# A Mamba/pooling decoder step on one core: the first gate tile multiplied from raw rows, and a new order of the first loads

## The chip, the cores and the metric

The kernel runs on one core of one Trainium2 chip. The metric is the device time of one execution in microseconds (us), the median of several runs. The engines are named as the profile names them: PE (TensorE, matmuls; PEld are its weight loads), DVE (VectorE), ACT (ScalarE), POOL (GpSimd) and SP (SyncE, which here only issues DMAs; SPq in the profile). Each engine runs its instructions in the order in which the program gives them, and waits for others at semaphores.

## The reference, cut to what matters

The model step has two layers, a Mamba-2 layer and a pooling layer, for 1024 prompt tokens and 8 samples of 8 tokens, 1088 tokens of 1024 features in all. Each layer first makes a modulated, normed input and projects it:

```
mod = silu(c) @ ada_w + ada_b;  shift, scale, gate = split(mod, 3)
hn  = rmsnorm(x, norm_g) * (1 + scale) + shift
zxbcdt = hn @ w_in            # z: 2048 gate columns, then x/B/C and dt
...                           # conv, state-space scan, y * silu(z), ...
```

`scale` and `shift` have one row for the prompt and one for each sample. Only the front of the first layer is touched: `mod` for layer 0, the norm, `hn`, and the first of the sixteen tiles (128 columns each) of `silu(z)`. All inputs and results are fp32.

## The kernel before, in words

Features lie on the 128 partitions and tokens along the free dimension, so `x` is eight tiles of 128x1088 (`xs[0]` to `xs[7]`). An exact product is made of three matmuls in the fp32r format: each operand is split in a rounded part (`hi`, ACT) and the rest (`lo`, DVE), and `mm1` (L182 to L186) adds hi*hi (L184), hi*lo (L185) and lo*hi (L186). A column tile of `w_in` against all of `hn` is thus 8 feature tiles x 3 token chunks (368, 368 and 352 columns) x 3 = 72 matmuls.

What the front does before the change, in its order:

- **Loads** (`setup`, L196, and `front`, L1338), all on SP's queue: the conditioning `cT`, the eight `x` tiles (L203), the constants `vec` and `kc` (L206, L208), the weight for dt (`wdt`), and then, two transfers each, the adaLN weights of layer 0 (`ada`, L251) in eight blocks, with the first weight tiles (`wr`, L121) behind the first block.
- **Warming**: 55 fp32 matmuls of 128 columns on a tile of ones (L220 calls `warm`, its matmul is L239).
- **1/rms**: ACT squares each `x` tile as it lands (L1347, L1351), DVE adds them up in `rst` (L1352), three fp32 matmuls with ones sum over the partitions (L295, tiles `ms`), and ACT makes 1/rms with Ln and Exp (L298, L311).
- **adaLN**: `ada_block` (L242) multiplies one block by the conditioning, as 2 x 4 fp32 matmuls in four column strips (L255, tiles `am`), copies the sum (L260), and picks nine columns with two more matmuls (L264). DVE then makes `shf` (L273) and `scl` (L274). One block gives shift and scale of one feature tile.
- **The loop over k** (L1372 to L1386 of `front`): for each of the eight feature tiles `modulate` (L313) makes `hn`: DVE multiplies by scale and 1/rms (L318), ACT adds the shift and rounds (L324, the hi part `hh`), DVE takes the rest (L325, `hl`), ACT writes `hn` back over `x` (L326), and the 64 sample tokens get their own small operations (L331 to L335). The 18 matmuls of two gate tiles (2 x 3 chunks x 3) and the dt matmuls (L1384) of that k follow. Gate tiles 0 and 1 so grow together in six PSUM banks.
- **Gate tiles 2 and 3** are then made one after the other (L1395 to L1402), 72 matmuls each. Meanwhile `act_sums_front` (L1405) makes the sums and differences of `hn` that the next stage needs (DVE subtractions at L1412, splits on ACT at L1415 and DVE at L1416), and `dt_phase` (L443) works on dt.
- **`front_pairs`** (L1446) makes all further tiles in pairs by seven half-size products instead of eight (`fast_pair`, L1022; matmuls L1017 to L1019, tiles `st`). The sums of weights for it are made by POOL (`w_sums`, L982 to L989), which also takes the rest of some splits (L178; ACT's rounding is L176). A raw weight tile (`wr`) is one of three buffers, and the next load into a buffer waits until its readers are done.

What sets the order around the change: the program order and `issue_after` marks feed a scheduler, so an engine's queue isn't the order of the code. In SP's queue a transfer that must wait holds up those behind it.

The lines of the program before that the steps below speak of most:

```
def ada_first(self, kt):                               # one block: shift and scale of tile kt
    for _ in self.ada_shift_scale(0, kt, False): pass
...
self.ada_first(0); ...; self.ada_first(1)              # ahead of the loop over k
for k in range(8):
    if k < 6: self.ada_first(k + 2)
```

## Time and profile before

| | |
|---|---|
| time, median of 3 runs | 1612.11 us (1608.94 to 1612.48) |
| the profiled execution | 1608.36 us; its span, first to last instruction, 1606.6 us |
| mean granted TensorE clock | 0.996 |
| PE busy | 1579.4 us (98% of the span) |
| DVE, ACT, POOL busy | 1292.8 us, 790.0 us, 506.7 us |
| first matmul of the exact product | 23.77 us after the span's start |
| last dt matmul group of the loop over k begins | 68.39 us |

The profile is one execution. All times within it count from the first instruction. "PE busy" counts a matmul from its start to its modelled end, so a full PE isn't a PE at its peak; where it waits shows in the idle time ahead of an instruction and in what ended it. The granted clock is that of PE, as a share of full speed.

### The profile page before, as it was taken

How to read it: one execution, taken by the hardware profiler on the slowest of the kernel's cores; microseconds unless marked ns; L12 is line 12 of the kernel's file. 1: busy time of each engine (PE TensorE's matmuls, PEld its weight loads, DVE VectorE, ACT ScalarE, POOL GpSimd, SP SyncE). 2: the span in 40 equal slices, each digit the busy share in tenths (PEclk: the TensorE clock that was granted, in tenths of full speed). 3: DMA queues.
4: the chain of work that ended last, by engine and by line, in shares of the span. 5: the costliest groups of instructions: out<-in, count | busy, mean ns of one | idle time of the engine just before them, and what ended most of it. 6: DMA issues, size and time to landing. Idle time of an engine off the chain costs nothing.

```text
span 1606.6 us, 30635 instructions
## 1 busy us (share of the span) xinstructions
PE 1579.4 (98%) x11916; PEld 1505.1 (94%) x11916; DVE 1292.8 (80%) x2148; ACT 790.0 (49%) x1511; POOL 506.7 (32%) x562
## 2 busy tenths in 40 slices
PE   8999999999999999999999999999999999999997
PEld 6899999998889889888899898999999999999997
DVE  6975779778888888888888967988889867677886
ACT  6663343447676666675545437632232233333364
POOL 0133556522221312130212222275666640000241
PEclk9999999999999999999999999999999999999999
DMA  9422232354555454768898632133323379565783
GB/s 351 166 100 84 95 111 71 109 185 150 198 166 174 151 199 144 245 214 303 287 330 292 221 133 86 57 131 114 115 101 101 116 232 364 161 171 177 161 177 119
DMA packets 122305, 275.58 MB, mean 172 GB/s; under 512 B 18192, under 2 KB 59312, under 8 KB 122160
## 3 DMA queue, kind: packets, MB, share of 16 engines
q1 hardware_dynamic: 118128, 260.90, 47.1%
q0 software_dynamic: 4032, 12.72, 4.5%
q8 instruction: 94, 1.54, 0.4%
q14 instruction: 51, 0.42, 0.1%
HBM read 201.12 MB, written 70.23 MB: 169 GB/s over the span
## 4 chain that ended last, share of the span: by engine, by line
PE 84%; DVE 6%; issue 4%; ACT 2%; DMA 2%; POOL 2%; SPq 0%; DVEq 0%; ACTq 0%; POOLq 0%
PE mm L184 11%; PE mm L185 10%; PE mm L186 10%; PE st L1019 10%; PE st L1017 10%; PE st L1018 10%; PE op L1234 3%; PE op L1235 3%; PE op L1233 3%; PE y L625 2%; PE S L604 2%; PE y L629 2%; PE tr L565 1%; PE am L255 1%; DVE xbc L352 1%
## 5 line engine op out<-in xcount | busy, mean ns | idle before, releaser
L1017 PE MATMUL st<-hh,w 128*128 128x272 f32 x832 | 240.3, 289 | 0.9 <-ACT w L176 0.9
L1019 PE MATMUL st<-hh,w 128*128 128x272 f32 x832 | 240.4, 289 | 0.4 <-DVE w L178 0.4
L1018 PE MATMUL st<-hl,w 128*128 128x272 f32 x832 | 240.0, 288 | 0.0
L1019 PE MATMUL st<-t,w 128*128 128x272 f32 x624 | 179.6, 288 | 1.7 <-POOL w L178 1.7
L184 PE MATMUL mm<-hh,wh 128*128 128x368 f32 (+1 forms) x528 | 179.3, 340 | 1.3 <-ACT raw L425 1.3
L1017 PE MATMUL st<-t,w 128*128 128x272 f32 x624 | 179.6, 288 | 0.0
L1018 PE MATMUL st<-t,w 128*128 128x272 f32 x624 | 179.2, 287 | 0.0
L185 PE MATMUL mm<-hl,wh 128*128 128x368 f32 (+1 forms) x528 | 174.4, 330 | 0.0
L186 PE MATMUL mm<-hh,wl 128*128 128x368 f32 (+1 forms) x528 | 173.9, 329 | 0.0
L1017 PEld LDWEIGHTS st<-hh,w 128*128 128x128 f32 x832 | 156.8, 188 | 1.3 <-ACT w L176 1.3
L1019 PEld LDWEIGHTS st<-hh,w 128*128 128x128 f32 x832 | 156.4, 188 | 0.9 <-DVE w L178 0.9
L1018 PEld LDWEIGHTS st<-hl,w 128*128 128x128 f32 x832 | 156.7, 188 | 0.0
L176 ACT ACTIVATE w<-wr 128x512 fp32r<-128x512 f32 x104 | 64.9, 629 | 166.7 <-PE st L1019 135.9
L612 POOL TENSOR_TENSOR hd<-h,cd 128x256 f32<-128x256 f32 x56 | 44.6, 797 | 319.5 <-DVE h L613 167.8
L1233 PE MATMUL op<-b,w 128*128 128x272 f32 x448 | 129.4, 289 | 0.0
L1234 PE MATMUL op<-b,w 128*128 128x272 f32 x448 | 128.8, 287 | 0.6 <-DVE b L1163 0.6
L1235 PE MATMUL op<-b,w 128*128 128x272 f32 x448 | 128.9, 288 | 0.0
L184 PE MATMUL mm<-gh,wh 128*128 128x368 f32 (+1 forms) x372 | 125.6, 338 | 0.5 <-DVE x L801 0.4
L185 PE MATMUL mm<-gl,wh 128*128 128x368 f32 (+1 forms) x372 | 122.2, 329 | 0.1
L186 PE MATMUL mm<-gh,wl 128*128 128x368 f32 (+1 forms) x372 | 122.2, 329 | 0.0
L1019 PEld LDWEIGHTS st<-t,w 128*128 128x128 f32 x624 | 117.3, 188 | 1.9 <-POOL w L178 1.9
L1017 PEld LDWEIGHTS st<-t,w 128*128 128x128 f32 x624 | 117.6, 189 | 0.1
(306 smaller groups left out, 4558.5 us busy)
## 6 DMA issues: line engine op xcount, KB each, us to landing
wr<-win SPq DMA_DIRECT2D x48, 512.0 KB, 5.3
acb<-acd SPq DMA_DIRECT2D x64, 256.0 KB, 4.6
wr<-pin SPq DMA_DIRECT2D x32, 512.0 KB, 4.0
wr<-pout SPq DMA_DIRECT2D x28, 512.0 KB, 4.6
x<-x1d SPq DMA_DIRECT2D x24, 544.0 KB, 6.1
x1d<-x SPq DMA_DIRECT2D x22, 544.0 KB, 5.1
wr<-pout POOLq DMA_DIRECT2D x20, 512.0 KB, 5.5
x<-xT SPq DMA_DIRECT2D x16, 544.0 KB, 7.2
```

What stands on the lines that cost most here:

```text
L176: self.nc.scalar.activation(hi, src, AF.Copy)
L184: nc.tensor.matmul(ps[:, :n], hi[:, k, :], ah[:, a:a + n], start=first, stop=False)
L185: nc.tensor.matmul(ps[:, :n], hi[:, k, :], al[:, a:a + n], start=False, stop=False)
L186: nc.tensor.matmul(ps[:, :n], lo[:, k, :], ah[:, a:a + n], start=False, stop=last)
L604: nc.tensor.matmul(S[:, 256 * i:256 * i + 256], Bt, xde.rearrange("p r q -> p (r q)"), start=True, stop=True)
L612: nc.gpsimd.tensor_tensor(out=hd, in0=h[-1], in1=cd.unsqueeze(2).to_broadcast([P, 4, 64]), op=ALU.mult)
L1017: nc.tensor.matmul(ps[c][:, :QUART], hi[:, k], xh[:, t], start=(k == 0), stop=False)
L1018: nc.tensor.matmul(ps[c][:, :QUART], hi[:, k], xl[:, t], start=False, stop=False)
L1019: nc.tensor.matmul(ps[c][:, :QUART], lo[:, k], xh[:, t], start=False, stop=(k == 3))
L1233: nc.tensor.matmul(ps[:, :QUART], hi[:, k], xh, start=k == 0, stop=False)
L1234: nc.tensor.matmul(ps[:, :QUART], hi[:, k], xl, start=False, stop=False)
L1235: nc.tensor.matmul(ps[:, :QUART], lo[:, k], xh, start=False, stop=k == 7)
```

## The change

Gate tile 0 (`win[4]`) leaves the loop over k. It is computed as

z0 = silu( rst * ( (scl * W0)^T x ) + W0^T shf )

with plain fp32 matmuls on the raw `x` tiles while these are still being loaded. The parts:

- **Loads.** A table `LOADS` sets the order on SP: only the columns of `vec` and `kc` that are needed at once, then a block of *scales*, `x`, a half of W0, and so on. A block of layer 0 now holds the scales of two feature tiles or the shifts of two (`ada0`), so four blocks are scales (first index 1) and four are shifts (0). Before the last `x` tile stand three scale blocks and W0; the fourth scale block and the first shift block follow it, then two `wr` tiles, a shift block, the rest of the constants (`consts`), `wdt` and the last two shift blocks.
- **The raw product** (`plain(k)`): DVE multiplies W0 by the scale (two tiles at a time, `ws0`) and the 64 sample columns of `x` by theirs (`x2`); PE does three fp32 matmuls per k (512, 512 and 64 columns), into three PSUM banks that gate tile 1 (now the second tile of the loop) took before. k = 0 to 5 come while `x` loads; k = 6 and 7 come after 1/rms in the code, since their scales are the last block.
- **Warming** is 16 matmuls at the start, 2 and 4 around the first block, and 3, 3 and 6 behind k = 1, 3 and 5.
- **Eviction**: DVE multiplies the three banks by `rst` into `z0`. Behind k = 6 of the loop, eight small matmuls (32 rows out), a copy, a 9-column matmul and two small DVE operations make W0^T shf; the Silu of the prompt columns takes it as its bias.
- **The loop over k** makes gate tiles 1 and 2, with three shift blocks in it (at k = 0, 2 and 4) instead of six full blocks. Only gate tile 3 is made behind it, and `act_sums_front` takes two of its steps per chunk of that tile instead of one.

The diff, cut to its core:

```
+LOADS = ((1, 0), ("x", 0), ("w", 0), ("x", 1), (1, 1), ("x", 2), ("w", 1), ("x", 3), (1, 2), ("x", 4), ("x", 5), ("x", 6), ("x", 7), (1, 3), (0, 0))
+WARM = 16
+FILLS = (3, 3, 6)
...
-        self.xs = []
-        for k in range(8):
-            t = self.slots.get("x")
-            nc.sync.dma_start(t, io["xT"][k])
-            self.xs.append(t)
         self.vec = cp.tile([P, V_N], F32, tag="vec", name="vec")
-        nc.sync.dma_start(self.vec, io["vec"])
         self.kc = cp.tile([P, K_N], F32, tag="kc", name="kc")
-        nc.sync.dma_start(self.kc, io["kc"])
+        nc.sync.dma_start(self.vec[:, :V_CW], io["vec"][:, :V_CW])
+        nc.sync.dma_start(self.kc[:, K_SEL9:K_SEL64], io["kc"][:, K_SEL9:K_SEL64])
+        self.xs, self.adaw = [], {}
+        self.w0 = self.slots.get("w0", extra=True)
+        for x, i in LOADS:
+            if x == "x":
+                t = self.slots.get("x")
+                nc.sync.dma_start(t, io["xT"][i])
+                self.xs.append(t)
+            elif x == "w":
+                nc.sync.dma_start(self.w0[:, 512 * i:512 * i + 512].rearrange("p (k m) -> p k m", k=4), io["win"][4][:, 4 * i:4 * i + 4])
+            else:
+                self.ada_load(x, i)
...
-        self.warm(55)
+        self.warm(WARM)
...
+    def consts(self):
+
+        nc, io = self.nc, self.io
+        nc.sync.dma_start(self.kc[:, :K_SEL9], io["kc"][:, :K_SEL9])
+        nc.sync.dma_start(self.kc[:, K_SEL64:], io["kc"][:, K_SEL64:])
+        nc.sync.dma_start(self.vec[:, V_CW:], io["vec"][:, V_CW:])
+        self.cwh = self.gp.tile([P, 160], F32, tag="cwh", name="cwh")
+        nc.vector.tensor_scalar(self.cwh, self.vec[:, V_CW:V_CW + 160], 0.5, None, op0=ALU.mult)
+
+    def warm(self, n, tag="mm", bufs=3):
+
...
-    def ada_first(self, kt):
-        for _ in self.ada_shift_scale(0, kt, False):
-            pass
+    def ada_load(self, s, j):
+        self.adaw[s, j] = raws = [self.slots.get("ada") for _ in range(2)]
+        for hh, t in enumerate(raws):
+            self.nc.sync.dma_start(t[:, :1024].rearrange("p (a b) -> p a b", a=4), self.io["ada0"][s, j][:, 4 * hh:4 * hh + 4, :])
+
+    def ada_first(self, s, j, fill=()):
+
+        nc = self.nc
+        blk = self.ada_block(self.adaw.pop((s, j)))
+        next(blk)
+        if fill:
+            self.warm(fill[0])
+        p2 = next(blk)
+        for i in range(2):
+            kt = 2 * j + i
+            if s:
+                nc.vector.tensor_scalar(self.scl[0][:, kt, :], p2[:, 16 * i:16 * i + 9], self.adab1[:, 8 + kt:9 + kt],
+                                        self.vec[:, V_NG + kt:V_NG + kt + 1], op0=ALU.add, op1=ALU.mult)
+            else:
+                nc.vector.tensor_scalar(self.shf[0][:, kt, :9], p2[:, 16 * i:16 * i + 9], self.vec[:, V_ADAB + kt:V_ADAB + kt + 1], None, op0=ALU.add)
+        if fill:
+            with self.tc.issue_after(self.sel):
+                self.warm(fill[1])
...
-        items += [(io["win"][i], 8) for i in (4, 5, 10, 11)]
+        items += [(io["win"][i], 8) for i in (5, 10, 11)]
...
+        banks = [[("mm", 3)] * 3, [("y", 2), ("y", 2), ("S", 1)]]
+        parts = ((0, 512), (512, 512), (NP, NS))
...
+        def plain(k):
+            scl = self.scl[0]
+            if k % 2 == 0:
+                nc.vector.tensor_tensor(out=ws0[:, k:k + 2], in0=w0[:, k:k + 2], in1=scl[:, k:k + 2, 8:9].to_broadcast([P, 2, P]), op=ALU.mult)
+            nc.vector.tensor_tensor(out=x2[:, k].rearrange("p (b i) -> p b i", i=8), in0=xs[k][:, NP:TOK].rearrange("p (b i) -> p b i", i=8),
+                                    in1=scl[:, k, 0:8].unsqueeze(2).to_broadcast([P, 8, 8]), op=ALU.mult)
+            for c, (a, n) in enumerate(parts):
+                w, x = (ws0[:, k], xs[k][:, a:a + n]) if c < 2 else (w0[:, k], x2[:, k])
+                ins = nc.tensor.matmul(ps0[c][:, :n], w, x, start=(k == 0), stop=(k == 7))
+            return ins
+
+        self.ada_first(1, 0, (2, 4))
...
+            for k in range(8):
+                if k < 6:
+                    ins = plain(k)
+                    if k in (1, 3, 5):
+                        with self.tc.issue_after(ins.ins):
+                            self.warm(FILLS[k // 2])
+                    if k in (0, 2):
+                        self.ada_first(1, k // 2 + 1)
+                square(k)
+            for i in range(2):
+                self.stream_raw(i)
+            self.ada_load(0, 1)
+            self.consts()
+            wdts = sl.get("wdt")
+            wdt = wdts[:, :256].rearrange("p (k m) -> p k m", k=8)
+            nc.sync.dma_start(wdt, io["wdt"])
             for a, n in CH:
                 self.ms_log(rst, rst, a, n, 1.0 / 1024, "mm", 3)
...
+        self.ada_first(1, 3)
+        plain(6)
+        self.ada_first(0, 0)
+        plain(7)
...
+        self.stream_split(0, True)
+        self.stream_split(1)
...
+        pst = [tiles(0)]
...
+            if k % 2 == 0 and k < 6:
+                if k < 4:
+                    self.ada_load(0, k // 2 + 2)
+                self.ada_first(0, k // 2 + 1)
-            if k == 6:
-                self.stream_split(3)
...
+            if k == 0:
+                for c, (a, n) in enumerate(parts):
+                    nc.vector.tensor_tensor(out=z0[:, a:a + n], in0=ps0[c][:, :n], in1=rst[:, a:a + n], op=ALU.mult)
+                pst.append(tiles(1))
...
+            if k == 6:
+                pb = self.pp.tile([P, 512], F32, tag="tr", bufs=2, name="pb")
+                for i in range(8):
+                    j = i % 4
+                    nc.tensor.matmul(pb[32 * j:32 * j + 32, :P], self.shf[0][:, i, :], w0[:, i], start=(i < 4), stop=(i >= 4), tile_position=(0, 32 * j))
+                mb = self.tp.tile([P, P], F32, tag="mb", name="mb")
+                nc.scalar.activation(mb, pb[:, :P], AF.Copy)
+                nc.tensor.matmul(pb[:, 256:265], mb, self.kc[:, K_SEL9:K_SEL9 + 9], start=True, stop=True)
+                bz = self.tp.tile([P, 9], F32, tag="bz", name="bz")
+                nc.vector.tensor_copy(bz, pb[:, 256:265])
+                zs = z0[:, NP:TOK].rearrange("p (b i) -> p b i", i=8)
+                nc.vector.tensor_tensor(out=zs, in0=zs, in1=bz[:, 0:8].unsqueeze(2).to_broadcast([P, 8, 8]), op=ALU.add)
...
+        nc.scalar.activation(z0[:, :NP], z0[:, :NP], AF.Silu, bias=bz[:, 8:9])
+        nc.scalar.activation(z0[:, NP:TOK], z0[:, NP:TOK], AF.Silu)
+        self.gate_store(0, z0)
+            self.gate_store(1 + i, dst)
         ops = self.act_sums_front()
-        for i in range(2):
-            w, dst = self.stream_next(), sl.get("z")
-            for c, ch in enumerate(CH):
-                ps = self.mm_tile()
-                self.mm3(ps, w, self.hn, ch)
-                with self.tc.issue_after(self.gate_chunk(dst, c, ps).ins), self.tc.issue_after(last.ins):
-                    next(ops)
-            self.gate_store(2 + i, dst)
+        w, dst = self.stream_next(), sl.get("z")
+        for c, ch in enumerate(CH):
+            ps = self.mm_tile()
+            self.mm3(ps, w, self.hn, ch)
+            ins = self.gate_chunk(dst, c, ps).ins
+            with self.tc.issue_after(ins) if c else contextlib.nullcontext(), self.tc.issue_after(last.ins):
+                next(ops)
+                next(ops)
+        self.gate_store(3, dst)
...
-    A["adaA"] = aw[:, :, :, :2].transpose(0, 4, 2, 1, 3, 5).reshape(2, 8, P, 8, 256)
+    A["ada0"] = aw[0][:, :, :2].reshape(8, P, 2, 4, 256).transpose(2, 3, 1, 0, 4)
+    A["adaA"] = aw[1][:, :, :2].transpose(3, 1, 0, 2, 4).reshape(8, P, 8, 256)
```

How the queues change at three places, as the instructions stand in them. Names carry running numbers; line numbers are those of the kernel concerned, so the changed kernel's differ from the ones above.

SP's queue from its first transfer, before (`x_1` to `x_8` are `xs[0]` to `xs[7]`):

```order
L199 DMA ct_175<-cT 128x72
L203 DMA x_1_177<-xT 128x1088
L203 DMA x_2_179<-xT 128x1088
L203 DMA x_3_181<-xT 128x1088
L203 DMA x_4_183<-xT 128x1088
L203 DMA x_5_185<-xT 128x1088
L203 DMA x_6_187<-xT 128x1088
L203 DMA x_7_189<-xT 128x1088
L203 DMA x_8_191<-xT 128x1088
L206 DMA vec_193<-vec 128x282
L208 DMA kc_195<-kc 128x778
L1344 DMA wdt_9_275<-wdt 128x256
```

The same queue in the changed kernel, from the second `x` tile on. Ahead of these rows stand `cT`, parts of `vec` and `kc`, the first scale block (`ada_2`, `ada_3`), the first `x` tile (`x_4`) and the first half of W0:

```order
L212 DMA x_5_189<-xT 128x1088
L293 DMA ada_6_191<-ada0 128x1024
L293 DMA ada_7_192<-ada0 128x1024
L212 DMA x_8_195<-xT 128x1088
L215 DMA w0_1_181<-win 128x512
L212 DMA x_9_198<-xT 128x1088
L293 DMA ada_10_200<-ada0 128x1024
L293 DMA ada_11_201<-ada0 128x1024
L212 DMA x_12_204<-xT 128x1088
L212 DMA x_13_206<-xT 128x1088
L212 DMA x_14_208<-xT 128x1088
L212 DMA x_15_210<-xT 128x1088
```

The last `x` tile moves from the ninth to the nineteenth place, with three scale blocks and W0 ahead of it and the rest of the constants behind it.

PE's queue around the start of the exact product, before: `ms` are the sums for 1/rms, `am` the first adaLN block, `mm` and `p` the two gate tiles of the loop.

```order
L295 MATMUL ms9_305<-rst_10_277,ones_197 128x368
L295 MATMUL ms10_309<-rst_10_277,ones_197 128x368
L295 MATMUL ms11_313<-rst_10_277,ones_197 128x352
L255 MATMUL am12_321<-ada_11_317,scp_202 32x256 x4
L255 MATMUL am12_321<-ada_12_319,scp_202 32x256 x4
L264 MATMUL am12_321<-kc_195,mp13_330 128x9 x2
L184 MATMUL mm18_367<-hh_21_393,w0_13_338 128x368
L184 MATMUL mm19_368<-hh_21_393,w0_13_338 128x368
L185 MATMUL mm18_367<-hl_22_394,w0_13_338 128x368
L186 MATMUL mm18_367<-hh_21_393,w0_14_339 128x368
```

The same place in the changed kernel, behind the three `ms` matmuls and the eight `am28` ones. `am28` is the fourth scale block, `am30` the first shift block, `am37` the second; `p02`, `p03` and `p04` are the three banks of the raw product, and `p034_461<-hh_31` is the first matmul of the exact product:

```order
L276 MATMUL am28_413<-kc_178,mp29_422 128x9 x2
L1400 MATMUL p04_260<-x2_21_262,w0_1_181 128x64
L267 MATMUL am30_433<-ada_19_217,scp_225 32x256
L1400 MATMUL p02_258<-x_14_208,w0_20_261 128x512
L1400 MATMUL p03_259<-x_14_208,w0_20_261 128x512
L267 MATMUL am30_433<-ada_19_217,scp_225 32x256 x3
L1400 MATMUL p02_258<-x_15_210,w0_20_261 128x512
L276 MATMUL am30_433<-kc_178,mp31_442 128x9 x2
L1400 MATMUL p03_259<-x_15_210,w0_20_261 128x512
L1400 MATMUL p04_260<-x2_21_262,w0_1_181 128x64
L267 MATMUL am37_469<-ada_23_390,scp_225 32x256 x4
L187 MATMUL p034_461<-hh_31_484,w0_27_453 128x368
```

The raw products of the last two feature tiles (`x_14`, `x_15`) now stand between the scale block's pick (the first row) and the exact product, and the first shift's pick (`kc_178,mp31`) stands between two of them.

POOL's queue from the first sums of weights, before. `wr43`, `wr47` and `wr48` are raw weight tiles, `sw52` and `sw73` sums of them, `w57` and `w65` parts for products, the `raw97` rows belong to dt:

```order
L982 TENSOR_TENSOR sw52_996<-wr47_892 128x512
L983 TENSOR_TENSOR sw52_996<-sw52_996,wr43_786 128x512
L987 TENSOR_TENSOR wr47_892<-wr43_786,wr47_892 128x512
L441 COPY raw97_1437<-raw64_1101 128x128
L441 COPY raw97_1437<-raw63_1100 128x128
L178 TENSOR_TENSOR w57_1012<-wr47_892,w57_1012 128x512
L989 TENSOR_TENSOR sw52_996<-wr43_786,sw52_996 128x512
L982 TENSOR_TENSOR sw73_1185<-wr68_1140 128x512
L441 COPY raw97_1437<-raw42_772 128x128
L983 TENSOR_TENSOR sw73_1185<-sw73_1185,wr48_894 128x512
```

The same in the changed kernel (`wr50`, `wr51`, `wr52`; `sw56`, `sw77`; `w61`, `w69`):

```order
L1015 TENSOR_TENSOR sw56_964<-wr51_836 128x512
L1016 TENSOR_TENSOR sw56_964<-sw56_964,wr50_834 128x512
L1020 TENSOR_TENSOR wr51_836<-wr50_834,wr51_836 128x512
L1022 TENSOR_TENSOR sw56_964<-wr50_834,sw56_964 128x512
L181 TENSOR_TENSOR w61_980<-wr51_836,w61_980 128x512
L1015 TENSOR_TENSOR sw77_1153<-wr72_1108 128x512
L1016 TENSOR_TENSOR sw77_1153<-sw77_1153,wr52_838 128x512
L1020 TENSOR_TENSOR wr72_1108<-wr52_838,wr72_1108 128x512
L181 TENSOR_TENSOR w69_1077<-wr51_836,w69_1077 128x512
```

The last sum into the first `sw` (`sw52` before, `sw56` now), which frees the buffer of the first weight tile, moves ahead of the first part for a product (`w57`, now `w61`), and the rows of dt move behind this piece.

63 lines of the change are left out of this document (27 added, 36 removed).

## The prediction

> **What bounds the kernel now.** I read the page first: its first part says which engine is full.
>
> ```profile
> span 1606.6 us, 30635 instructions
> PE 1579.4 (98%) x11916; PEld 1505.1 (94%) x11916; DVE 1292.8 (80%) x2148; ACT 790.0 (49%) x1511; POOL 506.7 (32%) x562
> ```
>
> PE is busy for all but 27 us, so a change is worth what it takes from PE's useful queue, or from the times in which PE has nothing to do. Both lie at the front. The next view is the table by stretches, cut where the front changes character.
>
> ```profile
> core 0: us, PE busy (x) PEld busy (x) DVE busy (x) ACT busy (x) POOL busy (x), PEclk, DMA share, GB/s
> 0.00:6.00 6.00, 4.94 (x23) 4.94 (x24) 0.88 (x5) 3.94 (x4) 0.51 (x5) 1.00 0.67 220
> 6.00:16.00 10.00, 9.98 (x89) 9.79 (x88) 7.31 (x6) 7.38 (x8) 0.00 (x0) 1.00 1.01 396
> 16.00:19.20 3.20, 2.01 (x6) 1.05 (x6) 2.36 (x8) 1.74 (x6) 0.00 (x0) 1.00 1.01 374
> 19.20:23.40 4.20, 1.91 (x21) 0.84 (x20) 2.43 (x12) 3.32 (x8) 0.00 (x0) 0.97 1.02 416
> 23.40:30.00 6.60, 5.90 (x23) 3.52 (x27) 4.93 (x10) 3.57 (x7) 0.00 (x0) 0.50 1.03 410
> 30.00:34.60 4.60, 4.15 (x43) 2.24 (x35) 2.06 (x5) 1.97 (x4) 0.00 (x0) 1.00 1.01 387
> 34.60:69.10 34.50, 34.47 (x287) 28.24 (x287) 30.31 (x54) 22.35 (x32) 4.88 (x3) 1.00 0.60 204
> 69.10:93.00 23.90, 23.90 (x146) 23.90 (x147) 21.31 (x39) 14.04 (x26) 0.84 (x2) 1.00 0.18 72
> 93.00:111.00 18.00, 16.29 (x130) 16.07 (x130) 16.71 (x25) 15.23 (x24) 10.21 (x7) 1.00 0.18 63
> ```
>
> Up to 16 us PE only warms (112 of the records are the 55 fp32 matmuls, two records each) and the DMA engines are full. Up to 23.4 us they still are, and PE does little. Then PE runs the exact product, 6.6 us of it at half the granted clock. From 34.6 to 93.0 us PE is full: the loop over k to 69.1 us, then gate tiles 2 and 3, 144 matmuls in 23.9 us, so **0.166 us per matmul and 11.95 us per tile**.
>
> What holds the start up is in the timeline (all engines, selected rows: start, duration, engine, line, operation, and in brackets the idle time and its releaser).
>
> ```profile
> 1.20 4.11 SPq L203 DMA_DIRECT2D x<-xT  x8
> 15.29 1.30 ACT L1351 ACTIVATE raw<-x 128x368 f32<-128x368 f32 x3 [0.25 <-DMA x<-xT]
> 17.19 2.10 PE L295 MATMUL ms<-rst,ones 128*128 128x368 f32 x6 [1.21 <-DVE rst L1352]
> 20.01 0.89 ACT L311 ACTIVATE rst<-rst 128x368 f32<-128x368 f32 x2
> 20.80 0.38 ACT L260 ACTIVATE mp<-am 128x256 f32<-128x256 f32 x1
> 22.17 0.28 DVE L274 TENSOR_SCALAR scl<-am,adab,vec 128x9 f32<-128x9 f32 x1
> 23.11 1.11 ACT L324 ACTIVATE hh<-x,shf 128x368 fp32r<-128x368 f32 x2 [0.75 <-DVE x L318]
> 23.77 1.19 PE L184 MATMUL mm<-hh,w 128*128 128x368 f32 x2 [1.92 <-ACT hh L324]
> ```
>
> The last `x` lands at 15.3 us; 1/rms is ready at 20.9 us, 5.6 us later; the scale at 22.45, the first `hh` at 23.7, the first exact matmul at 23.77.
>
> **The change, part by part.** I follow four terms against the profiled execution.
>
> *(1) The first exact matmul.* By the DMA groups, with the kilobytes of each transfer,
>
> ```profile
> x<-xT SPq DMA_DIRECT2D x16, 544.0 KB, 7.2
> ada<-adaA SPq DMA_DIRECT2D x16, 512.0 KB, 9.8
> ```
>
> what must arrive up to the last `x` is 8 x 544 + 6 x 512 + 2 x 256 + about 80 KB = 8.2 MB, against 4.5 MB before. Adding up the last column of the stretches (1.32 MB by 6 us, 5.28 by 16, 6.48 by 19.2, 8.22 by 23.4) this queue has moved 8.2 MB at 23.4 us. In the same sum the 4.5 MB of `x` are in at 14.0, but the last square starts at 15.29: 1.3 us until a transfer counts as landed. The first large transfer is issued behind three small ones instead of one; SP spends about 0.45 us on each, so add 0.9 us. The last `x` then lands at **25.6 us**, 10.3 later.
>
> PE meanwhile has 16 raw 512-column products. One warm fp32 matmul of 128 columns takes 9.98 / 89 x 2 = 0.224 us in the second stretch; four times that is 0.9 us. The three `ms` give 2.10 / 1088 columns, so at most 1.0. With a short 64-column one a k costs 2.0 us. The six that come while `x` loads are 12 us in a gap of some 18, so the loads pace them, and DVE, busy 7.31 of 10 us there, has room for the scaling multiplies (eight of some 0.2 us, four of some 0.4); but the third scale block lands at about 20.5 us by the same sums (6.0 MB at 17.9, plus 2.2, taken as up to 2.6). Block, copy, pick, scale and the weight multiply take some 2.5 us (19.2 to 22.45 before, less the wait for the second half), so k = 4 and 5 run from 23.0 to 26.8, and the six warm matmuls behind them end at 28.15. These stand in PE's queue ahead of `ms`, whose first chunk is ready at 27.0: **1.1 us is lost there**. From `ms` to the end of Exp took 3.7 us before (17.19 to 20.90), so 1/rms is ready at about 31.9.
>
> ACT's queue holds the copy of the fourth scale block behind Exp, so the scale comes at 33.5 (mp to scale: 1.65 us above, and here a hop more), the scaled weights at 34.1. Then, on the path, k = 6 and most of k = 7 of the raw product (3 x 0.9 us, and 0.35 of `am30`) stand ahead of the first shift's pick: 37.15. The pick, `shf` and `hh` take 1.7 (21.23 to 23.7 before, less the DVE multiplies, which are done early here). First exact matmul at **38.9 us, 15.1 later**. Bounds: with the loads at the best rate of a row (416 GB/s throughout) it would be 2 us earlier; if the first landings keep the 220 GB/s of the first six microseconds for another ten, 4 later. I take the rate of the rows as they follow each other, since the queue is as full as then.
>
> *(2) From there to the end of the loop over k.* Before: 23.77 to 69.1, 45.3 us, with half clock and waits in its first 11. Now: 144 matmuls x 0.166 = 23.9, and from the chain of waits
>
> ```profile
> 45.27 0.68 PE pdt L1384 x8
> 45.95 0.86 PE am L255 x16
> 47.67 0.34 PE am L264 x4
> ```
>
> eight dt groups, 5.4; three shift blocks of 1.2, 3.6, with 0.1 for each switch; the bias product, nine small matmuls, about 0.8: 34.0 us. Waits: DVE must do the second weight split, `hl` in three chunks and the eviction of the raw product before the banks of gate tile 2 are free, and the second shift's pick waits for a copy that ACT does behind `hh` of k = 1. I count 1.1 us. Later DVE needs per k
>
> ```profile
> L318 DVE SCALAR_TENSOR_TENSOR x<-x,scl,rst 128x1024 f32<-128x1024 f32 x7 | 9.0, 1280 | 0.1
> L325 DVE SCALAR_TENSOR_TENSOR hl<-x,shf,hh 128x1024 fp32r<-128x1024 f32 x7 | 9.0, 1279 | 1.5 <-ACT hh L324 1.5
> L335 DVE TENSOR_TENSOR hl<-x,hh 128x64 fp32r<-128x64 f32 x8 | 1.7, 226 | 0.0
> ```
>
> 2.56 plus four small ones, 3.2 to 3.5 us, against PE's 2.99 + 0.68 = 3.67. DVE keeps ahead, but barely; without that cover each k would cost what DVE lacks. Sum 35.1 us, the loop ends at **74.0** (69.1 before). Bounds for the waits: none (72.9), or PE idle until DVE has finished all of k = 0, some 4 us (77).
>
> *(3) Behind the loop* one tile is left instead of two: **-11.95 us**. Its cover: in 69.1 to 93.0 DVE is busy 21.3 us and from 93 to 111 another 16.7, with `act_sums_front` and dt. That must now fit in 12 us less. It does if the rest of dt is late: behind the reciprocal, dt's chain stands after the first evictions of the pair stage, 7 us of DVE work.
>
> *(4) The wait in the first pair.* PE waits once between 60 and 150 us:
>
> ```profile
> PE st L1019 <- POOL w L178: 1.7, 1, 1.7
> ```
>
> and the timeline of POOL shows what that part waited for:
>
> ```profile
> 96.21 2.32 POOL L178 TENSOR_TENSOR w<-wr,w 128x512 fp32r<-128x512 f32 x1 [5.24 <-ACT w L176]
> 98.47 1.75 POOL L989 TENSOR_TENSOR sw<-wr,sw 128x512 f32<-128x512 f32 x1
> 103.73 1.79 POOL L982 TENSOR_TENSOR sw<-wr 128x512 f32<-128x512 f32 x1 [3.51 <-DMA wr<-win]
> 108.67 1.25 POOL L178 TENSOR_TENSOR w<-wr,w 128x512 fp32r<-128x512 f32 x1
> ```
>
> The buffer of a weight tile comes free only after L989, which stood behind a part that waits for ACT; the load, a sum and the part needed follow. In the new order that sum comes before the part, so the load waits for nothing on POOL, only for the store of gate tile 3 ahead of it on SP. It would land at about 90 us, the part be ready at 96, and PE want it at 104. **-1.7 us**; bounds 0 and -1.7.
>
> Sum: +15.1 - 10.2 - 11.95 - 1.7 = **-8.75 us**, 1608.36 to 1599.6 in the profiled execution's terms. The median shown is 3.75 us above that execution; I subtract from the median and forecast **1603.4 us**. The case's own range, with the bounds added, is 1600 to 1607. From the tail of the pair stage on, the order is the same and PE full, so what is gained stays.
>
> **The rivals.**
>
> *Half clock again.* Between the end of `am30`'s first half (30.6) and the first raw product of k = 6 (34.1) PE has 0.5 us of work. Before, the same kind of pause (19.2 to 23.4, 1.91 busy of 4.2) was followed by 6.6 us at 0.50. If it comes, the raw products of k = 6 and 7 take 1.8 us each instead of 0.9: 3 x 0.9 = 2.7 us on the path, and little behind it, since PE waits there anyway: saved 6.1, **1606.0 us**. Against it: the pause is a little shorter, and `ms` and warming lie just ahead of it. Chance 0.25.
> [...]
>
> *The handover.* DVE had 4.8 + 21.3 + 16.7 = 42.8 us of work from its first difference (64.3) to 111 us, and would have about 37. If the dt chain can't be put off, it is 5.8 us late, less what PE doesn't need: 4 us, and the 1.7 stay: saved 3, **1609.1**. For it: DVE is at 9 tenths there. Chance 0.13.
>
> *The raw product isn't hidden.* If PE is at half clock through the loads, 12 x 1.8 = 21.6 us start at 10, `ms` comes 3.5 us later, k = 6 and 7 another 2.7, and gate tile 0 is largely paid for after all: saved 2.5, **1609.6**. Against it: the warm matmuls between. Chance 0.06.
>
> *Slower: the stream ahead of the last `x`.* 3.7 MB stand newly ahead of it. If its transfers mixed with smaller pieces keep the 220 GB/s of the first stretch, the last `x` lands at 8.2 / 0.22 + 2 = 39 us, 13.7 after my 25.6: 5 us **slower, 1617**. It decides above 34.4 us, 8.75 later than I say, a mean rate of 260 GB/s. The rows give 374 to 416 with `ada` in flight. Chance 0.07.
>
> **The numbers.** Forecast 0.49, half clock 0.25, handover 0.13, not hidden 0.06, slower 0.07. A difference of 0.2% (3.2 us) is about what can be told from none. Faster by more: the first two and half of the handover, 0.80; within: the rest of it and most of the third, 0.12; slower 0.08. The range is 1598 (early loads, and a median as low as the lowest run shown) to 1610.5, leaving out the slower rival and a part of the third.
>
> **What would show it.** In the new profile: the last square starts at about 25.6; the first exact matmul at about 39; the granted clock between 30 and 40; the last dt group ends near 74; the first `st` matmul at about 86; no wait of PE for POOL's part behind it. A last `x` after 34, a first exact matmul after 48, or PE waiting for DVE's splits beyond 86 would make the forecast wrong.

## The result, and the profile after the change

The change made the kernel **slower**: 1617.42 us in the median (1616.18 to 1619.51, 6 runs) against 1610.3 us (1608.94 to 1612.48, 6 runs) for the kernel before, a ratio of 1.0046 with a 95% interval of 1.0036 to 1.0056. I had forecast 1603.4.

The profiled execution took 1617.07 us, its span is 8.7 us longer than before. The first lines of its page:

```profile
span 1615.3 us, 30555 instructions
PE 1586.7 (98%) x11868; PEld 1500.0 (93%) x11868; DVE 1297.7 (80%) x2164; ACT 785.3 (49%) x1508; POOL 506.6 (31%) x563
```

PE is as full as it was, so the share says nothing of the loss: PE is busy for 7.3 us longer, in a span that is 8.7 us longer. The table by stretches, cut at the events that the prediction named:

```profile
core 0: us, PE busy (x) PEld busy (x) DVE busy (x) ACT busy (x) POOL busy (x), PEclk, DMA share, GB/s
16.00:24.00 8.00, 7.07 (x40) 3.74 (x40) 3.54 (x7) 2.49 (x3) 0.00 (x0) 1.00 1.03 415
24.00:27.00 3.00, 1.66 (x16) 0.97 (x15) 0.95 (x5) 2.11 (x3) 0.00 (x0) 1.00 1.03 411
27.00:34.00 7.00, 7.00 (x25) 3.95 (x25) 5.49 (x9) 2.46 (x5) 0.00 (x0) 0.76 1.02 408
34.00:45.67 11.67, 10.38 (x67) 4.92 (x65) 7.71 (x17) 6.11 (x12) 0.00 (x0) 1.00 0.85 327
45.67:84.20 38.53, 37.49 (x282) 28.75 (x279) 34.02 (x70) 24.47 (x37) 4.71 (x3) 1.00 0.27 96
84.20:96.20 12.00, 12.00 (x74) 12.00 (x74) 11.09 (x18) 10.07 (x19) 0.00 (x0) 1.00 0.36 141
96.20:130.00 33.80, 33.43 (x264) 33.00 (x264) 31.86 (x49) 19.61 (x35) 15.65 (x12) 1.00 0.29 102
130.00:135.00 5.00, 1.73 (x13) 1.29 (x11) 4.45 (x10) 1.70 (x3) 3.81 (x6) 0.89 0.13 36
135.00:142.00 7.00, 7.00 (x37) 7.00 (x37) 4.13 (x14) 1.08 (x2) 0.74 (x6) 0.59 0.13 52
```

Two places are new. From 16 to 45.67 us PE is busy for most of the time, so the front is not mainly a wait for loads. And at 130 us, where PE was full before, it stops for 3.3 us, and then runs at 0.59 of the clock for 7 us more.

Set beside the prediction, with the moments of the two profiles:

| | before | forecast | after |
|---|---|---|---|
| `ms` starts | 17.19 | 28.15 | 33.85 |
| first exact matmul | 23.77 | 38.9 | 45.67 |
| loop over k ends | 69.1 | 74.0 | 84.2 |
| first `st` | 92.8 | 86 | 96.2 |
| last `st` of the front's pairs | 350.7 | | 359.2 |
| end of the span | 1606.6 | 1597.85 | 1615.3 |

So of the 17.4 us between forecast and result 6.8 are lost ahead of the first exact matmul, 3.4 in the loop over k (38.5 us instead of 35.1), none in gate tile 3 (12.0 us), and 6.8 in the pairs (263.0 us from the first to the last `st`, 257.9 before, 1.7 less forecast); the rest is rounding and 0.2 us behind the pairs, where both kernels take the same (1255.9 us before, 1256.1 after).

**The front.** The timeline of the changed kernel (all engines, selected rows):

```profile
18.50 4.04 PE L1400 MATMUL p<-x,w 128*128 128x64 f32 x10 [0.78 <-DVE x L1396]
23.31 0.89 PE L255 MATMUL warm<-ones 128*128 128x128 f32 x6
24.13 0.64 PE L267 MATMUL am<-ada,scp 128*32 128x256 f32 x8
24.89 0.38 ACT L272 ACTIVATE mp<-am 128x256 f32<-128x256 f32 x1 [5.72 <-PE am L267]
25.17 4.28 ACT L1388 ACTIVATE raw<-x 128x1088 f32<-128x1088 f32 x6
26.72 5.90 PE L1400 MATMUL p<-x,w 128*128 128x64 f32 x12 [0.78 <-DVE x L1396]
31.25 1.36 DVE L1390 TENSOR_TENSOR rst<-rst,raw 128x368 f32<-128x368 f32 x3
32.46 1.56 PE L255 MATMUL warm<-ones 128*128 128x128 f32 x12
33.85 1.99 PE L328 MATMUL ms<-rst,ones 128*128 128x368 f32 x6
36.57 0.89 ACT L344 ACTIVATE rst<-rst 128x368 f32<-128x368 f32 x2
40.10 1.98 PE L1400 MATMUL p<-x,w 128*128 128x512 f32 x4
44.87 2.56 ACT L357 ACTIVATE hh<-x,shf 128x368 fp32r<-128x368 f32 x4 [0.78 <-DVE shf L309]
45.67 0.78 PE L187 MATMUL p<-hh,w 128*128 128x368 f32 x2
```

PE does not wait for the third scale block (the `am` at 24.13 has no idle time ahead of it). It comes to it late, because the raw product of k = 2 and 3 stands ahead. ACT has nothing to do for 5.72 us: in its queue the squares of `x[4]` to `x[7]` stand behind the copy of that block, and DVE's sums behind its scales. All four squares then run back to back. The raw product of k = 4 and 5 takes 5.90 us instead of 4, with a granted clock of 0.50 from 29 to 31.5 us, and `ms` comes behind it and the warm matmuls.

**The pairs.** The waits of PE between 60 and 150 us, and the timeline of the dt chain on DVE with the row of PE that needs it:

```profile
PE tr L536 <- DVE tka L534: 2.7, 1, 2.7
PE tr L533 <- DVE z L1061: 0.6, 1, 0.6
PE st L1052 <- DVE w L181: 0.2, 1, 0.2
```

```profile
102.52 0.48 DVE L497 TENSOR_TENSOR raw<-raw,raw 128x320 f32<-128x320 f32 x1
114.71 0.47 DVE L498 TENSOR_TENSOR raw<-raw 128x320 f32<-128x320 f32 x1
124.15 1.81 DVE L509 TENSOR_TENSOR_SCAN raw<-kc,raw 128x320 f32<-128x320 f32 x1
132.19 1.56 DVE L181 TENSOR_TENSOR w<-sw,w 128x512 fp32r<-128x512 f32 x1 [0.55 <-ACT w L179]
134.37 0.47 DVE L534 COPY tka<-tr 128x128 f32<-128x128 f32 x2
134.79 0.45 PE L536 MATMUL tr<-kc,raw 128*128 128x128 f32 x1 [2.71 <-DVE tka L534]
```

Before the change the scan of this chain ran at 89.5 us:

```profile
89.53 0.82 DVE L476 TENSOR_TENSOR_SCAN raw<-kc,raw 128x320 f32<-128x320 f32 x1
```

Now it runs at 124, and the transposes (`tr`) that read its result have kept their place in PE's queue, ten rows among the products of the second pair. PE reaches them at 130 us. The first two wait 0.6 us at most. The long wait, 2.7 us, is the next one's: DVE must first copy out what the first two have made (`tka`), and in DVE's queue that copy stands behind a split (`w`) that starts only at 132.19, after a wait for ACT. Everything behind the transposes in PE's queue stops meanwhile.

### The profile page after: what moved, and what is told of

Its sections match the earlier page's. It is cut to its first block, busy times and chain, and to the rows that moved or that the text cites. A ratio compares the mean times of both kernels' runs of the same rounds, so it can differ in the third digit from the quotient of the medians.

```text
span 1615.3 us, 30555 instructions
## 1 busy us (share of the span) xinstructions
PE 1586.7 (98%) x11868; PEld 1500.0 (93%) x11868; DVE 1297.7 (80%) x2164; ACT 785.3 (49%) x1508; POOL 506.6 (31%) x563
## 4 chain that ended last, share of the span: by engine, by line
PE 78%; DVE 6%; issue 4%; ACT 2%; DMA 2%; POOL 1%; DVEq 0%; SPq 0%; ACTq 0%; POOLq 0%
PE mm L187 10%; PE mm L188 10%; PE mm L189 10%; PE st L1052 10%; PE st L1050 9%; PE st L1051 9%; PE op L1267 2%; PE op L1268 2%; PE op L1266 2%; PE y L658 2%; PE S L637 2%; PE y L662 2%; PE tr L598 1%; DVE xbc L385 1%; PE am L267 1%
## 5 line engine op out<-in xcount | busy, mean ns | idle before, releaser
L187 PE MATMUL mm<-hh,wh 128*128 128x368 f32 (+1 forms) x504 | 171.6, 341 | 1.3 <-ACT raw L458 1.3
L188 PE MATMUL mm<-hl,wh 128*128 128x368 f32 (+1 forms) x504 | 166.6, 330 | 0.0
L189 PE MATMUL mm<-hh,wl 128*128 128x368 f32 (+1 forms) x504 | 166.0, 329 | 0.0
```

The lines of the kernel that those rows point to most:

```text
L187: nc.tensor.matmul(ps[:, :n], hi[:, k, :], ah[:, a:a + n], start=first, stop=False)
L188: nc.tensor.matmul(ps[:, :n], hi[:, k, :], al[:, a:a + n], start=False, stop=False)
L189: nc.tensor.matmul(ps[:, :n], lo[:, k, :], ah[:, a:a + n], start=False, stop=last)
```

## The experiments

My theory after the profile: the time is lost in two places that have nothing to do with each other, the order of PE's queue ahead of the first exact matmul, and the transposes of dt. The rivals: the loads set the front; DVE as a whole sets the pairs, whatever PE's order; or PE's own added work sets the front. All ratios below are to the kernel before on the same chip; the changed kernel's is 1.0046.

### 1. The transposes one pair later

```
-                if n < 2 and x in ("B21", "T3", "T4"):
+                if (n, x) in ((0, "B21"), (0, "T3"), (0, "T4"), (1, "B21"), (2, "T3")):
                     next(dt, None)
```

> The changed kernel with one edit: the ten transposes at the end of the dt chain come one pair later in PE's program (behind the third half product of the third pair instead of the second pair). Theory A (the dt chain runs late on DVE, so PE's queue stops at its transposes at 132 us, and a slower clock follows): the stall of 3.3 us and the clock at 0.50 from about 135 to 142 us both go, 5.8 us in all, and the median comes to about 1611.5. Rival B (DVE as a whole is the bound from 97 to 135 us, and the transposes only stand where its lateness shows): the stall moves to the half products that wait for their operands, and at most 1.5 us are gained, about 1616. Rival C (the time is lost only in front of 84 us): no difference.

1612.62 us (11 runs), ratio 1.0008 (0.9999 to 1.0017): 0.38%, or 6.1 us, gained. The same two stretches of this kernel:

```profile
130.00:135.00 5.00, 5.00 (x42) 5.00 (x42) 4.45 (x7) 3.57 (x6) 4.92 (x5) 1.00 0.24 93
135.00:142.00 7.00, 7.00 (x58) 7.00 (x58) 6.38 (x14) 2.91 (x5) 1.71 (x2) 1.00 0.33 105
```

PE is full and at full clock, with DVE no less busy than it was. Theory A holds: the place of ten small matmuls, not the sum of DVE's work, made the stop. From the first to the last `st` it is 256.8 us, less than before the change. (The front of this execution was slower than the changed kernel's, with `ms` at 35.90 us, though the edit does not touch it: k = 2 and 3 ran in part at half clock too, 5.73 us, with a mean of 0.84 from 20 to 30 us.)

### 2. The third scale block ahead of k = 3

```
                 if k < 6:
-                    ins = plain(k)
+                    with self.tc.issue_after(self.sel) if k == 3 else contextlib.nullcontext():
+                        ins = plain(k)
```

> The changed kernel with one edit: PE does the third scale block, and its pick, between k = 2 and k = 3 of the raw product instead of behind k = 3. Theory A (PE's queue order, not the loads, makes the third block late; ACT's squares and DVE's sums of the later x tiles stand behind its copy and its scales): the copy comes at about 21.5 us instead of 24.9, k = 4 starts at about 24 instead of 26.7, the squares run as x lands, ms starts at 28 to 30 instead of 33.85, and the first exact matmul comes at about 41 instead of 45.7; of these 4.7 us some 4 show in the time, about 1613. Rival B (the loads: the last x lands only when the squares now run, about 28): the first exact matmul moves by under 1 us, about 1617. Rival C (PE is bound by its own work ahead of the first exact matmul, and only its pauses can go): 2 to 3 us, about 1614.5.

1613.48 us (12 runs), ratio 1.0020 (1.001 to 1.003): 0.26%, 4.2 us. In the profiled execution k = 2 ran at half clock this time (3.68 us for its two large matmuls instead of 2), so the copy came at 23.8 us and not at 21.5, `ms` at 32.60 and the first exact matmul at 42.98, 2.7 us earlier. The direction is that of theory A; the first exact matmul moved by as much as C said, the time by as much as A. What the loads allow was seen in full only when the clock was kept up (experiment 8).

### 3. The first shift block ahead of k = 6 and 7

```
-        plain(6)
         self.ada_first(0, 0)
-        plain(7)
+        for k in (6, 7):
+            with self.tc.issue_after(self.sel):
+                plain(k)
```

> The changed kernel with one edit: PE does the first shift block and its pick ahead of the raw product of k = 6 and 7 instead of between. Theory A (from 1/rms on, a chain of copy, pick and shift sets the first exact matmul, and PE has slack): hh is ready at about 40 instead of 44.9, the first exact matmul at about 42 instead of 45.7, and the time falls by 2 to 3.5 us, about 1614.5. Rival B (PE has to do the raw product of k = 6 and 7 anyway, 4.4 us, so only its 1.3 us of pauses between 37 and 40 us can go): at most 1 us, 1616.5 or no difference, the raw product then ending as late as before.

1611.61 us (11 runs), ratio 1.0011 (1.0002 to 1.0019): 0.35%, 5.6 us, more than either theory said. From `ms` to the first exact matmul it is 10.0 us instead of 11.8, and to the end of the loop 2.5 us less: theory A's size. In the profile the first exact matmul came at 45.46 and not at 42, because `ms` started 1.6 us later than in the changed kernel, at 35.43: half clock came twice ahead of it (k = 2 and 3 took 5.67 us and k = 4 and 5 5.90; the mean is 0.84 from 20 to 30 us and 0.88 from 30 to 40). The rest is an effect that I had not meant: the stop at the transposes was 1.7 us instead of 2.7, and the clock stayed at 1.00 behind it, so the pairs took 258.4 us instead of 263.0.

### 4. Without the six warm matmuls

```
-FILLS = (3, 3, 6)
+FILLS = (3, 3, 0)
```

> The changed kernel with one edit: the six warm matmuls behind k = 5 of the raw product are left out (they compute nothing that is used). Theory A (ms waits behind them on PE from 32.6 to 33.85 us): ms starts at about 32.6 and all that follows comes 1.2 us earlier, about 1616.2. Rival B (they hold up the granted clock): the clock falls again between 33 and 38 us, and the raw product of k = 6 and 7 takes up to 4 us longer: about 1619.

1617.13 us (5 runs), ratio 1.0042 (1.003 to 1.0054), no difference. Both theories were half right: `ms` starts at 32.48, 1.4 us earlier, and then the clock falls during k = 6 (a mean of 0.84 from 30 to 40 us), whose two large matmuls take 3.48 us instead of 1.98. The first exact matmul comes at 46.00 instead of 45.67.

### 5. The warm matmuls in the pauses

```
-FILLS = (3, 3, 6)
+FILLS = (0, 0, 6)
...
-                        self.ada_first(1, k // 2 + 1)
+                        self.ada_first(1, k // 2 + 1, (2, 3))
```

> The changed kernel with its six warm matmuls behind k = 1 and 3 of the raw product moved: three each now stand behind the pick of the second and of the third scale block, where PE pauses for 0.8 us before k = 2 and k = 4. Theory A (the half clock in the raw product follows PE's pauses at 17 to 18.5 and 24 to 26.7 us, and costs 1.5 us each time it comes): with the pauses filled k = 2 to 5 run at full clock in every execution, ms starts 1.5 to 3 us earlier than in the same execution of the changed kernel (31 to 32.5), and the median falls by 1.5 to 2 us, to about 1615.7. Rival B (the clock does not hang on these pauses, each too short): the clock still falls to 0.5 between 20 and 32 us, no difference.

With `(2, 3)` there are ten warm matmuls where six were: in the trace two more run behind the first block, five behind the pick of the second and three behind that of the third.

1615.96 us (6 runs), ratio 1.0034 (1.0022 to 1.0046): 0.12%, which is theory A's size but hardly more than the measurement tells. The profile is clearer: k = 2 to 5 ran at full clock (1.00 from 10 to 30 us), `ms` started at 31.27, 2.6 us earlier. Then the clock fell in k = 6 (3.10 us instead of 1.98, a mean of 0.91 from 30 to 40 us), behind the next pause.

### 6. POOL's sums later

```
+        t = self.tp.tile([P, 1], F32, tag="gate", name="gate")
+        ins = self.nc.gpsimd.tensor_copy(t, self.hn[5][1][:, :1].bitcast(F32))
+        with self.tc.issue_after(ins.ins):
             self.wahead = [w for w in itertools.islice(self.wgen, 3)]
```

> The changed kernel with POOL's sums of the first pair's weights held back by one small copy on POOL that reads the hl of k = 5: they run at about 73 to 78 us instead of 49.5 to 54.3. Theory A (DVE's operations of 1.28 us take 2.2 to 2.3 beside POOL's sums, and 0.22 takes 1.3, and this makes PE wait in the loop over k): DVE's two operations at 50 to 55 us take 1.28 again, PE's wait of 1.0 us at 54.6 us goes, the loop ends about 1 us earlier, and the time falls by 1 us, about 1616.4; DVE's differences at 75 to 80 us get slower in their place. Rival B (the long durations have another cause, ACT or the loads at that time): they stay at 2.2 us, no difference.

1617.27 us (5 runs), ratio 1.0039 (1.0025 to 1.0053), no difference in the time. The effect on DVE is shown all the same. DVE's operations at 50 to 55 us took 1.27 and 0.21 us, and the slow ones went with POOL to 67 to 72 us. First DVE's rows in the changed kernel (POOL's sums run from 49.55 to 54.3), then those of this one (POOL from 67.0 to 72.0):

```profile
49.77 2.17 DVE L358 SCALAR_TENSOR_TENSOR hl<-x,shf,hh 128x1024 fp32r<-128x1024 f32 x1
51.86 1.32 DVE L365 TENSOR_TENSOR x<-x,scl 128x64 f32<-128x64 f32 x1
53.10 2.32 DVE L358 SCALAR_TENSOR_TENSOR hl<-x,shf,hh 128x1024 fp32r<-128x1024 f32 x1
```

```profile
50.90 1.28 DVE L358 SCALAR_TENSOR_TENSOR hl<-x,shf,hh 128x1024 fp32r<-128x1024 f32 x1
68.49 2.32 DVE L351 SCALAR_TENSOR_TENSOR x<-x,scl,rst 128x1024 f32<-128x1024 f32 x1
70.73 1.31 DVE L368 TENSOR_TENSOR hl<-x,hh 128x64 fp32r<-128x64 f32 x1
```

(They ran earlier than I had written, since hl of k = 5 is ready at 66.7 us.) PE's wait of 1.0 us for DVE in the loop went, with 0.4 left at another place, and the end of the loop was 0.9 us closer to `ms`; the stop at the transposes stayed at 2.7 us. So this is a cause of late DVE work, but at most 1 us of the 8.7.

### 7 and 8. Three and four edits together

The edits of 1, 2 and 3; then that of 5 as well.

> The edits of the first, second and third experiment together (transposes one pair later; third scale block ahead of k = 3; first shift block ahead of k = 6 and 7). Theory A (three separate losses): the handover stall is worth 4.8 to 5.8 us, the two edits in the front 2 to 3 us each: 4.8 + 2.5 + 2.5 = 10 us off 1617.4, about 1607.5, faster than the kernel before by 3 us. Rival B (they overlap, since a shorter front only moves the wait to DVE's work at 97 to 125 us, which is full there): no more than the best single one, about 1611.5, and PE waits for DVE's splits between 97 and 125 us.

> The last one with the warm matmuls moved into the pauses as well. Theory A: the raw product runs at full clock throughout, first exact matmul at about 39 to 40, and 1 to 2 us less than with three edits, about 1606. Rival B (the pauses are gone already with the third block ahead of k = 3, and the half clock with them): no difference from the three edits.

1612.77 us (12 runs, ratio 1.0011, 0.9999 to 1.0023) and 1613.28 us (12 runs, ratio 1.0014, 1.0003 to 1.0024). Both theories missed: the gains did not add up, and not because DVE's splits were late. PE's waits of the three edits between 84 and 120 us, and the stretches there:

```profile
PE st L1052 <- POOL w L181: 2.1, 1, 2.1
```

```profile
110.00:115.00 5.00, 2.86 (x22) 2.65 (x22) 5.00 (x8) 0.63 (x1) 3.79 (x3) 0.97 0.04 10
115.00:120.00 5.00, 5.00 (x30) 5.00 (x30) 5.00 (x14) 1.09 (x2) 0.00 (x0) 0.69 0.30 100
```

It is the wait for POOL's part of the kernel before, with a granted clock of 0.69 behind it. The edit of experiment 3 had turned round two neighbouring rows of POOL (the part L181 and the sum L1022 that frees the weight buffer), which the change itself had put the other way. The pairs take 259.8 us, 3.0 more than with the later transposes alone.

That explains a part of number 7, and nothing of number 8. There the same wait is 2.1 us as well, but the clock stays at 1.00 behind it and the pairs take 257.7 us. The last `st` starts at 349.5 us, 9.7 us ahead of the changed kernel and 1.2 ahead of the kernel before: up to there the gains did arrive. Behind it come 1260.6 us, where the changed kernel has 1256.1 and the one before 1255.9. None of the four edits touches the code there, and there is one profile of each kernel, so it is not shown whether the new order or only this execution makes that stretch longer. Why the gains do not add up in the medians stays open.

The four edits show where the loads stand. ACT's squares of the last two `x` tiles, at last with the loads as their releaser:

```profile
24.74 1.11 ACT L1388 ACTIVATE raw<-x 128x1088 f32<-128x1088 f32 x1 [0.25 <-DMA x<-xT]
26.10 1.29 ACT L1388 ACTIVATE raw<-x 128x368 f32<-128x368 f32 x3 [0.24 <-DMA x<-xT]
```

The last `x` lands at 26.1 us, half a microsecond behind the forecast. The raw product ran at full clock throughout (1.00 from 10 to 50 us), `ms` started at 30.75, and the first exact matmul came at 40.8, within 2 us of the forecast.

### 9. POOL's rows exchanged in the kernel before

```
-            yield self.split_half(z[:, f])
-            nc.gpsimd.tensor_tensor(out=s[:, l], in0=u[:, l], in1=s[:, l], op=ALU.subtract)
+            ins = nc.gpsimd.tensor_tensor(out=s[:, l], in0=u[:, l], in1=s[:, l], op=ALU.subtract)
+            with self.tc.issue_after(ins.ins):
+                w = self.split_half(z[:, f])
+            yield w
```

> The kernel before with two neighbouring rows of POOL exchanged in each pair where its order allows it (in the first pair the last sum of weights comes ahead of the part that waits for ACT); every other engine's order is unchanged. Theory A (as the prediction's fourth step had it: the load of the next weight tile waits for that sum alone): the load comes 2 us or more earlier, PE's wait of 1.7 us for POOL's part in the first pair goes, and the time falls by up to 1.7 us, to about 1608.8. Rival B (the load then waits for something else, the stores of gate tiles ahead of it on SP, or the sum waits for DVE's split): the wait stays at over 1 us and the time as it is, 1610.5.

1610.09 against 1610.07 us, ratio 0.9998 (0.9989 to 1.0007). PE's wait there fell from 1.7 to 0.7 us, and the pairs of the profiled execution took 256.8 us instead of 257.9. The time shows nothing of it, but the interval is too wide for 1 us in 1610. POOL's sum now waited 6.5 us for DVE's split and came only 1.1 us earlier against the first `st`: between A and B, and too small to see.

### 10 to 12. All edits, a better front, and that front alone

Number 10 is the four edits with POOL's rows as in 9. Number 11 is the same with another order from the last `x` on:

```
-            for a, n in CH:
-                self.ms_log(rst, rst, a, n, 1.0 / 1024, "mm", 3)
-                self.rstd(rst[:, a:a + n])
-        self.ada_first(1, 3)
+            self.ada_first(1, 3, (3, 0))
+            with self.tc.issue_after(self.sel):
+                for a, n in CH:
+                    self.ms_log(rst, rst, a, n, 1.0 / 1024, "mm", 3)
+                    self.rstd(rst[:, a:a + n])
         plain(6)
         self.ada_first(0, 0)
-        plain(7)
+        with self.tc.issue_after(self.sel):
+            plain(7)
```

Number 12 is the front of 11 without the later transposes and without POOL's rows.

> The changed kernel with the four edits (transposes later, third block ahead of k = 3, shift block ahead of k = 6 and 7, warm matmuls in the pauses) and POOL's exchanged rows. Theory A (with the first four, what was left over the kernel before was the wait of 2.1 us for POOL's part at 104 to 113 us and the slower clock behind it): the wait goes, 2 to 3.5 us less than the 1613.3 with four edits, about 1610, level with the kernel before. Rival B (DVE, full from 97 to 125 us, sets the pace there whatever POOL does): the wait comes back as one for DVE's splits, under 1 us gained, about 1612.5.

> As the last one, but the fourth scale block and its pick stand ahead of the sum over the partitions (ms), k = 6 of the raw product right behind it, and only k = 7 behind the first shift block; the warm matmuls behind k = 5 are three, ahead of that block. Theory A (from the last x on, PE has work for all the time up to the first exact matmul, and only the order makes it pause): the first exact matmul comes at about 37 to 38 us instead of 40 to 41, PE idle for under 1 us between 24 us and there, and the time falls by 2 to 3 us more, about 1607.5, faster than the kernel before. Rival B (the fourth block has not landed by then, and PE waits for it ahead of ms): the first exact matmul comes later than 41, the time is 1 us or more above the last one.

> The last experiment's front alone (third block ahead of k = 3, fourth ahead of ms, warm matmuls in the pauses), with the transposes of dt and POOL's rows as in the changed kernel. With the other three runs this makes a square of two edits: changed kernel 1617.4, transposes alone 1612.6, both 1608.05 (with POOL's rows). Theory A (the two losses are separate: DVE is full from 97 to 125 us whenever the handover comes, and the transposes stand too early for it): the stop at the transposes stays at 2.5 us or more, and the time is 1608.05 + 4.8, about 1612.9. Rival B (with the handover 4 us earlier DVE has caught up by the transposes): the stop is under 1 us and the time about 1609.5. Where the stop comes ahead of POOL's part, PE's wait for that part does not show.

| | median us (runs) | ratio to before |
|---|---|---|
| 10 | 1611.91 (11) | 1.0011 (1.0000 to 1.0022) |
| 11 | 1608.05 (11) | 0.9988 (0.9979 to 0.9997) |
| 12 | 1611.43 (12) | 1.0015 (1.0007 to 1.0024) |

Number 10 missed its theory A (1610): by the ratios it is no different from number 8. In its profile PE waits

```profile
PE st L1054 <- POOL w L181: 0.8, 1, 0.8
```

instead of 2.1 us, and the pairs take 257.6 us, as in 8 (257.7). Rival B's sign, PE waiting for DVE's splits, is not there either beyond 0.2 us. So the wait for POOL's part alone does not explain why the gains did not add up.

Number 11 is faster than both kernels, by 2 us over the one before and 9.3 over the changed one. Its first exact matmul did not come at 37 to 38 us but at 40.87, as in 10. What PE did up to there and in the loop:

```profile
24.00:27.00 3.00, 3.00 (x10) 1.51 (x9) 2.90 (x5) 2.51 (x3) 0.00 (x0) 1.00 1.03 411
27.00:34.00 7.00, 6.44 (x42) 3.89 (x41) 3.76 (x10) 2.09 (x6) 0.00 (x0) 1.00 1.03 412
34.00:40.87 6.87, 6.37 (x42) 3.15 (x40) 5.81 (x10) 5.83 (x12) 0.00 (x0) 1.00 1.03 398
40.87:79.78 38.91, 38.71 (x282) 28.62 (x278) 34.53 (x71) 24.22 (x36) 4.94 (x3) 1.00 0.33 122
```

PE idles for 1.1 us of the 17 from 24 us on. So the third rival of experiment 2, PE bound by its own added work, is what remains when the order is good: eight k of 2.0 us, four and a half blocks of 1.5, `ms` with 2, and the warm matmuls between fill some 27 of the 30 us from 11 to 41. The raw product alone is 16 us, more than the 11.95 of the tile that it replaces, so it pays only as far as it lies in time that PE had free. And at the end of the loop (79.78) the kernel stands only 1.3 us better than the one before, whose third of four gate tiles ends at 81.05.

What 11 has over 10 is no shorter path in the front: first exact matmul, clock (1.00 up to 45 us in both) and pairs are alike, and the last `st` starts at 348.9 and 349.4 us. The profiled executions differ by 7.3 us, and 6.8 of these lie behind the pairs (1255.4 and 1262.2 us), in code that is the same in both. The runs of 11 lie closer together, between 1606.1 and 1609.9 us, those of 10 between 1608.7 and 1617.9. What makes this difference is not shown. The mean granted clock goes with the time in some kernels (with three edits, number 7, the five runs at 0.994 have a median of 1615.0 us, the three at 0.997 one of 1609.1), but the two profiled executions here have 0.998 and 0.997.

Number 12 completes the square: the transposes alone gain 0.38%, the front alone 0.31%, both with POOL's rows 0.58%. The stop at the transposes is still 2.1 us in 12 with the loop ending 4 us earlier, and PE's wait for POOL's part another 2.1, so the two losses are separate in the main, as theory A of 12 said. 12 came out 1.5 us better than its sum, and the wait for POOL's part, which I had said would not show, did.

## Why the prediction was wrong, step by step

*The loads were right.* 8.2 MB by 25.6 us was the forecast, 26.1 us the measurement (experiment 8). The slower rival that I wrote down, a slow stream, is refuted. That it gave 1617, the time that was measured, is chance.

**Step 1 failed where it says "the loads pace them".** I compared 12 us of raw product with a gap of 18 us and took the rest as free. But the scale blocks, their picks and the raw products stand in one queue of PE, and each round of two k (block, copy, pick, scale, weights, 4 us of product) waits for the one ahead: rounds began at 10.56, 18.50 and 26.72 us. The third block was forecast at 20.5 us from its bytes, and PE took up its second half at 24.13, behind k = 2 and 3. Because I took the loads for the pace, I did not look at what stands behind a block's copy in ACT's queue: four squares, and behind its scales DVE's sums. `ms` was late by 5.7 us. Of these 3.7 are the order: k = 4 started at 26.72 and not at 23.0. The other 2 are half clock in k = 4 and 5. The warm matmuls ahead of `ms`, the only delay that I had seen, were in the forecast already. Moving one pick ahead gave back 4.2 us of time (experiment 2), and all of the front's order with the warm matmuls in its pauses 5.0 (experiment 12). The other 1.1 us up to the first exact matmul lie in the pick of the first shift block, which stood behind k = 6 (experiment 3).

*Half clock came, in another place.* I had priced it for k = 6 and 7. In the changed kernel it came in k = 4 and 5, behind 3 us in which PE was busy for 1.66, and in other executions in k = 2 or k = 6. So the front does not take a fixed time: up to `ms` the changed kernel and experiment 1 have the same front, and k = 2 and 3 took 4.04 us in the one and 5.73 in the other. What makes the clock fall behind a pause in one execution and not in another is not shown.

**Step 2 was mis-sized by 3.4 us**, nearly the same in every variant (38.5 us in the changed kernel, 38.9 in number 11, where PE is busy for 38.7). The dt groups mark the pace of the changed kernel's loop:

```profile
66.16 0.75 PE L1458 MATMUL pdt<-x,wdt 128*32 128x256 f32 x8
71.35 0.75 PE L1458 MATMUL pdt<-x,wdt 128*32 128x256 f32 x8
75.19 0.75 PE L1458 MATMUL pdt<-x,wdt 128*32 128x256 f32 x8
```

A k without extras takes 3.84 us, not 3.67 (71.35 to 75.19). The forecast had added 3.67 up from its parts; the chain of the kernel before has the 3.84 as it stands, in the last three k of its loop:

```profile
60.71 0.68 PE pdt L1384 x8
64.55 0.68 PE pdt L1384 x8
68.39 0.68 PE pdt L1384 x8
```

A k with a shift block takes 1.35 us more (66.16 to 71.35), not 1.2 and 0.1 for the switch. Over eight k and three blocks these are 1.5 us. The other 2 lie in the first three k, which take 17.3 us where the later rate gives 14.2. DVE is slow beside POOL there (2.17 and 2.32 us for operations that take 1.28 without it) and PE waits 1.0 us, but I had counted 1.1 us of waits, so waiting is not the excess; moving POOL's sums away took 0.9 us off the loop (experiment 6), and what makes the rest is not shown. "DVE keeps ahead, but barely" was the right worry with a small price.

*Step 3 was right in its number* (12.0 us for a tile) *and wrong in its cover.* I wrote that the work on DVE "does if the rest of dt is late" and did not ask who waits for dt. The answer was in the order of instructions: the transposes stand in PE's queue in the second pair, they had not moved, and PE stopped there for 3.3 us and ran at 0.59 of the clock for 7 more. The rival that I called the handover (0.13) had the mechanism, at 4 us; the pairs took 5.1 us longer than before. Putting the transposes later gave 6.1 us (experiment 1).

*Step 4 was right in its mechanism, and its worth cannot be told.* In the changed kernel PE's wait for POOL's part is gone, as forecast. In the kernel before, the exchange took 1.0 of the 1.7 us from the wait, too little for the time to show (experiment 9). In 7, 8 and 12 the old order of the two rows brought it back.

What I did not consider at all is that several of the rivals can come together. I gave each the forecast's other steps. The result has two of them together, half clock (in another place) and handover, and beside them two losses that were not on the list, the order of PE's queue and the loop's own rate.
